# Gated heads: each token's own score from an elementwise product on GpSimd and sums over two columns, in place of whole blocks times the identity

## The chip, the cores and the metric

The kernel runs on one core of a Trainium2 chip. The core has TensorE (matmuls, PE in the profile; its weight loads are PEld), VectorE (DVE), ScalarE (ACT), GpSimd (POOL) and SyncE (SP), which issues DMAs. TensorE writes to PSUM, eight banks of 128 partitions by 2 KB; the other data lie in SBUF. The engines run each their own list of instructions in order and wait for one another through semaphores. The metric is the device time of one execution in microseconds (us), the median of several runs.

## The reference, cut to what matters

The model is a two-layer decoder trunk on 512 tokens and 16 meta tokens (528 rows, width 1024). Each layer has a mixer of four retention heads and four gated heads (GLA, key width 64), then a gated MLP. The change is in the gated heads' scores within a sub-chunk:

```python
ddiff = cs[..., :, None, :] - cs[..., None, :, :]
dec = jnp.exp(jnp.where(causal[:, :, None], ddiff, -jnp.inf))
diag = jnp.einsum('bhnasd,bhnatd,bhnastd->bhnast', qs, ks, dec)
```

A query's score with an earlier key is weighted by the decays that lie between them. For a token with itself the decay is exp(0) = 1, and the score is just the sum over the 64 key elements of q times k, with no gate in it. That score, one number per token and head, is what the change computes in another way.

## The kernel before, in words

Activations are kept transposed: features on the 128 partitions, the 528 tokens along the free dimension. Weights come by DMA into a staging tile (`st`), and each block of 128 columns is split into two fp16 parts, the high one by ScalarE (L122) and the low one by VectorE (L126); both make a `unit`. A projection is 24 matmuls of such units with the fp16 parts of the input (`product_step`, L471 to L473), once for 232 and once for 296 tokens, into a PSUM tile `pj`. ScalarE takes it out (L1018), or for retention's q and k the rotary code on VectorE and ScalarE (L836 to L839).

The gated heads come in two pairs per layer; a pair lies on the 128 partitions as two heads of 64 (k in `kT`, q in `qT`, both in the tile `room`). For each pair `gla` is a generator that `mixer` starts once the last q is there (`done`), and whose pieces are interleaved with the projections: `gla_decay` makes the per-token decay `a` on ScalarE and VectorE (L902 to L909); `gla_scores` makes the scores; `gla_states` and `head_out` make the outputs.

`gla_scores` works in seven levels. The scores of a token with itself come first: for each head, keys against queries of the same 128 tokens as whole 128x128 blocks (`d0`, in PSUM, L955; for the 16 meta tokens `ptl`), of which VectorE keeps the diagonal by a product with the identity (L957 into `dg`, L958 into `dt`). Then q is multiplied by `a` (L960). At every level, token blocks double in length: ScalarE and VectorE write an fp16 split of the tile of keys and queries, `lvx` (L977, L978); GpSimd and VectorE multiply keys and queries by the decay of the neighbouring block (L980, L982); VectorE makes the decay products of the next level in `tots` (L985); TensorE multiplies the level's keys and queries (`lps`, L925), and VectorE copies the results under a mask over their place in `dg` and `dt` (L934, L938).

After the opening of layer 0, Tile's scheduler decides the order of instructions on each engine and inserts the waits. PSUM tiles rotate through the eight banks: `mm` has three buffers, `mx` five, and a matmul into a new tile waits until the last reader of the bank is done. SBUF tiles of 2112 bytes per partition rotate through 41 slots (`g`). `v_natural` transposes the values on TensorE into `ptv` (L746), between the projections.

Of the kernel before, what the change touches and what calls it, by code (L numbers as in the profile page):

```python
# [9 lines left out]
F32 = mybir.dt.float32  # L10
U8 = mybir.dt.uint8
AF = mybir.ActivationFunctionType
ALU = mybir.AluOpType

P = 128
NMETA = 16
SEQ = 512
L = NMETA + SEQ
D = 1024
KD = D // P  # L20
# [34 lines left out]
NROW = 84  # L55
# [20 lines left out]
def cell(pool, shape, dt, tag, name, bufs=None):  # L76

    n = math.prod(shape[1:])
    size = 2 if dt == F16 else 4
    t = pool.tile([shape[0], -(-n * size // CELL) * CELL // size], dt, tag=tag, name=name, **({"bufs": bufs} if bufs else {}))[:, :n]  # L80
    names = "abcdef"[: len(shape) - 1]
    return t if len(names) == 1 else t.rearrange(f"p ({' '.join(names)}) -> p {' '.join(names)}", **dict(zip(names, shape[1:])))
# [136 lines left out]
class Kern:  # L219
# [111 lines left out]

    def constants(self):
        nc, a, c = self.nc, self.a, self.const
        widths = (("h", KD * L), ("xroom", KD * L), ("ident", P), ("ones", P), ("mhalf", 10), ("par", NROW), ("pars", 48), ("cvec", 4 * 88), ("ss", 10), ("first", 10),
                  ("w2", 256), ("rank", KD * 16), ("tri", P), ("mask", len(LEVELS) * 16), ("decay", 2 * NH * 5 + 1), ("sso", 8), ("rooms", sum(n * c for _, n, c in KINDS)))
        every = cell(c, [P, sum(n for _, n in widths)], F32, "every", "every")
        at = 0
        for nm, n in widths:
            setattr(self, nm, every[:, at : at + n])
            at += n  # L340
        self.h = self.h.rearrange("p (k n) -> p k n", k=KD)
        self.mask = self.mask.bitcast(U8).rearrange("p (l c) -> p l c", l=len(LEVELS))
        self.heads = self.decay
        self.decay, self.early = self.heads[:, :-1].rearrange("p (a h c) -> p a h c", a=2, h=NH), self.heads[:, -1:]
        self.ring(self.rooms, KINDS)
        nc.gpsimd.memset(self.ones, 1.0)
        nc.gpsimd.memset(self.mhalf, -0.5)

    def first_gains(self, r0):
        nc = self.nc  # L350
        pt = self.mx([P, 16], "ptc")
        nc.tensor.transpose(pt, r0[:16, :], self.ident[:16, :16])
        nc.vector.tensor_copy(self.par[:, 0:16], pt)
        nc.vector.tensor_scalar(out=self.pars[:, 0:16], in0=pt, scalar1=SX, scalar2=None, op0=ALU.mult)
# [582 lines left out]
                m4 = self.mask[:16, li, :8].rearrange("p (b l) -> p b l", l=lv)  # L937
                nc.vector.copy_predicated(o4, m4, pst.rearrange("p (b l) -> p b l", l=lv))  # L938

    def gla_scores(self, kq, a, res):  # L940

        nc = self.nc
        kT, qT = kq[:, 0, :], kq[:, 1, :]
        dg = [self.g([P, 4, P], F32, "dg") for _ in range(2)]
        dt = self.sm([P, 2, P], "dgt")
        idb = self.ident[:, None, :].to_broadcast([P, 4, P])
        pss, ptl = [self.mx([P, 4, P], "d0") for _ in range(2)], [self.mx([P, 16], "ptl") for _ in range(2)]  # L950
        for c, (c0, w) in enumerate(HEADS):
            for h in range(2):
                hs = slice(64 * h, 64 * h + 64)
                dst = pss[h][:, c - 1, :] if c else ptl[h]
                nc.tensor.matmul(dst, kT[hs, c0 : c0 + P], qT[hs, c0 : c0 + w], start=True, stop=True)  # L955
        for h in range(2):
            nc.vector.tensor_tensor(out=dg[h], in0=pss[h], in1=idb, op=ALU.mult)  # L957
            nc.vector.tensor_tensor(out=dt[:NMETA, h, :NMETA], in0=ptl[h][:NMETA], in1=self.ident[:NMETA, :NMETA], op=ALU.mult)  # L958
        yield
        nc.vector.tensor_tensor(out=qT, in0=qT, in1=a, op=ALU.mult)  # L960
        tots = self.g([P, L], F32, "tots")
        tot, toff = a, 0
        xs = {}
        for step in range(len(LEVELS) + 1):
            if step < len(LEVELS):
                lv = LEVELS[step]
                at = 0 if lv <= 8 else NMETA
                n = L - at
                nb = n // (2 * lv)
                if lv == NMETA:  # L970
                    tot = tot[:, 1:]
                v = lambda t: t.rearrange("p (b two l) -> p b two l", two=2, l=lv)
                x = xs[step] = self.g([P, 2, n], F16, "lvx")
                k0 = v(kT[:, at:])
                p0, b0, t0, l0 = [list(d) for d in k0.ap]
                both = bass.AP(tensor=k0.tensor, offset=k0.offset, ap=[p0, b0, [L + lv, 2], l0])
                nc.scalar.activation(v(x[:, 0]), both, AF.Copy)  # L977
                nc.vector.tensor_tensor(out=v(x[:, 1]), in0=both, in1=v(x[:, 0]), op=ALU.subtract)  # L978
                t2 = tot[:, : n // lv].rearrange("p (b two) -> p b two", two=2)
                nc.gpsimd.tensor_tensor(out=k0[:, :, 0, :], in0=k0[:, :, 0, :], in1=t2[:, :, 1:2].to_broadcast([P, nb, lv]), op=ALU.mult)  # L980
                q1 = v(qT[:, at:])[:, :, 1, :]
                nc.vector.tensor_tensor(out=q1, in0=q1, in1=t2[:, :, 0:1].to_broadcast([P, nb, lv]), op=ALU.mult)  # L982
                tn = tots[:, toff : toff + nb]
                toff += nb
                nc.vector.tensor_tensor(out=tn, in0=t2[:, :, 0], in1=t2[:, :, 1], op=ALU.mult)  # L985
                tot = tn
            if step > 0:
                self.level_scores(step - 1, xs.pop(step - 1), dg, dt)
            yield LEVEL / PACE[0]
        res["kn"], res["tot"] = self.k_natural(kT), tot  # L990
        res["in"] = [lambda i, h=h: dg[h][:, i - 1, :] if i else dt[:, h, :] for h in range(2)]
        yield

    def mixer(self, l):
        nc = self.nc
# [11 lines left out]
        out, vnat, gates = {}, {}, {("gr", h): [None] for h in range(4)} | {("rg", h): [None] for h in range(4)}  # L1007
# [15 lines left out]
        kq = [room[:, 2 * L * pr : 2 * L * (pr + 1)].rearrange("p (i n) -> p i n", i=2) for pr in range(2)]  # L1023
# [4 lines left out]

        def gla(pr):
            res = {}  # L1030
            yield from self.gla_decay(*logits[pr], res)
            if pr:
                yield from self.pause(2)
            yield from self.gla_scores(kq[pr], res["a"], res)
            heads = (2 * pr, 2 * pr + 1)
            yield from self.pause()
            while any(("gv", hd) not in vnat for hd in heads):
                yield "waits"
            yield from self.gla_states(res["kn"], res["tot"], [vnat["gv", hd] for hd in heads], res)
            self.spawn(self.head_out([(res["in"][h], kq[pr][64 * h : 64 * h + 64, 1, :], res["sn"][64 * h : 64 * h + 64], vnat["gv", hd],  # L1040
                                       R_GLA + 4 * l + hd, gates["gr", hd], 4 + hd, None) for h, hd in enumerate(heads)]))
# [16 lines left out]
        def done(nm, h):  # L1058
            if (nm, h) == ("gq", 1):
                logits.extend(self.gate_logits(l, gaT))  # L1060
                self.gated.extend([gla(0), gla(1)])
            elif nm in ("gv", "rv"):
                self.spawn(vtr((nm, h)))
            elif nm == "rq":
                self.spawn(ret(h))
            elif nm in gates_n:
                gates[nm, h][0] = out[nm, h]
# [436 lines left out]
```

## Time and profile before

| | |
|---|---|
| median of 3 runs | 1232.73 us (1232.47 to 1232.76) |
| profiled execution | 1231.38 us |
| its span, first to last instruction | 1229.3 us |
| mean granted TensorE clock | 0.998 |
| busy in the span: TensorE / VectorE / ScalarE / GpSimd | 1209.6 / 869.0 / 676.5 / 161.8 us |

The profile page gives busy times, groups of instructions by line and what they waited for; the timeline gives start and duration of single instructions. A row such as `73.49 0.26 PE L471 MATMUL pj<-every,unit ... x1 [1.18 <-DVE dg L957]` reads: at 73.49 us into the span a matmul of line 471 started, writing the tile pj; the engine had stood idle for 1.18 us, until VectorE's instruction of line 957 was done. Matmuls are pipelined, so what one costs is read from start to start and not from its duration. A matmul in fp32 stands as two records. x16 and the like counts records that follow one another. The four places of the change lie at 67 to 77 us and 83 to 86 us (layer 0) and at 680 to 689 us and 696 to 698 us (layer 1).

### The profile page before, as it was taken

Reading aid. Unit: us, or ns where it says so; the run is one execution under the profiler, and the core shown is the slowest. Engines: PE = TensorE matmul, PEld = TensorE weight load, DVE = VectorE, ACT = ScalarE, POOL = GpSimd, SP = SyncE. Lnnn points to the kernel's source line nnn. Section 1 sums busy time; section 2 is a strip of 40 time slices with the busy share of each in tenths; the row PEclk is TensorE's granted clock in tenths of the full one; section 3 lists DMA queues with packets and bytes.
Section 4 is the critical chain, followed back from the end, with each engine's and each line's share of the span. In section 5 each row is a group of like instructions: output and inputs, shape, how many; then the busy total and the mean of one; then the engine's idle time right before and its main releaser. Section 6 shows DMA issues by size and latency. Waiting matters only on the chain.

```text
span 1229.3 us, 26444 instructions
## 1 busy us (share of the span) xinstructions
PE 1209.6 (98%) x11031; PEld 1012.3 (82%) x11031; DVE 869.0 (71%) x1541; ACT 676.5 (55%) x1337; POOL 161.8 (13%) x211
## 2 busy tenths in 40 slices
PE   8999999999999999999999999999999999999997
PEld 7778889979888888888887788899798888886444
DVE  5677845367998889623465878443779998887686
ACT  6675445454776666523336654453548766664452
POOL 2012311152000000000230123011520000000001
PEclk9999999999999999999999999999999999999999
DMA  8933221131422423424242332212303353305471
GB/s 210 269 103 87 67 73 53 52 103 36 137 70 70 122 86 109 141 80 103 63 113 68 104 87 70 75 48 70 114 8 104 103 172 103 121 1 172 151 251 69
DMA packets 207259, 124.17 MB, mean 101 GB/s; under 512 B 6992, under 2 KB 194692, under 8 KB 207140
## 3 DMA queue, kind: packets, MB, share of 16 engines
q1 hardware_dynamic: 206372, 121.23, 34.0%
q8 instruction: 86, 1.41, 0.5%
q10 hardware_dynamic: 608, 0.73, 0.2%
q0 software_dynamic: 160, 0.52, 0.1%
q14 instruction: 33, 0.27, 0.1%
HBM read 120.37 MB, written 2.10 MB: 100 GB/s over the span
## 4 chain that ended last, share of the span: by engine, by line
PE 82%; DVE 9%; ACT 4%; issue 2%; POOL 1%; DMA 1%; SPq 0%; POOLq 0%; DVEq 0%; ACTq 0%
PE pl L1345 8%; PE pu L472 8%; PE pu L473 8%; PE pu L471 8%; PE pj L471 7%; PE pj L473 7%; PE pj L472 7%; PE pp L1164 5%; PE pd L471 3%; PE pd L473 3%; PE pd L472 3%; PE po L471 2%; PE po L473 2%; PE po L472 2%; DVE unit L126 1%
## 5 line engine op out<-in xcount | busy, mean ns | idle before, releaser
L472 PE MATMUL pu<-every,unit 128*128 128x296 f16 (+2 forms) x1120 | 306.1, 274 | 2.6 <-DVE every L410 2.6
L473 PE MATMUL pu<-every,unit 128*128 128x296 f16 (+2 forms) x1120 | 306.1, 274 | 0.0
L471 PE MATMUL pu<-every,unit 128*128 128x296 f16 (+2 forms) x1120 | 304.5, 274 | 0.7 <-ACT every L409 0.7
L473 PEld LDWEIGHTS <-unit 128*128 128x128 f16 x2572 | 251.7, 98 | 42.0 <-issue 3.4
L471 PEld LDWEIGHTS <-unit 128*128 128x128 f16 x2572 | 252.3, 98 | 41.1 <-issue 3.0
L472 PEld LDWEIGHTS <-unit 128*128 128x128 f16 x2572 | 252.1, 98 | 39.2 <-issue 3.0
L126 DVE SCALAR_TENSOR_TENSOR unit<-st,unit 128x1024 f16<-128x1024 f32 (+1 forms) x165 | 201.6, 1225 | 84.3 <-ACT unit L122 83.7
L471 PE MATMUL pj<-every,unit 128*128 128x296 f16 (+2 forms) x888 | 244.4, 276 | 3.0 <-ACT gv L1018 1.6
L473 PE MATMUL pj<-every,unit 128*128 128x296 f16 (+2 forms) x888 | 244.2, 275 | 0.9 <-DVE unit L126 0.9
L472 PE MATMUL pj<-every,unit 128*128 128x296 f16 (+2 forms) x888 | 244.3, 275 | 0.0
L122 ACT ACTIVATE unit<-st 128x1024 f16<-128x1024 f32 x163 | 169.7, 1042 | 77.5 <-PE pd L473 22.7
L437 DVE TENSOR_TENSOR acc<-acc,sq 128x296 f32<-128x296 f32 (+2 forms) x60 | 32.9, 550 | 75.8 <-ACT sq L435 74.0
L1164 PEld LDWEIGHTS <-unit 128*128 128x128 f16 x756 | 73.9, 98 | 13.3 <-issue 2.3
L473 PE MATMUL pd<-av,unit 128*128 128x232 f16 (+1 forms) x308 | 84.7, 276 | 0.0
L472 PE MATMUL pd<-av,unit 128*128 128x232 f16 (+1 forms) x308 | 84.7, 276 | 0.0
L471 PE MATMUL pd<-av,unit 128*128 128x296 f16 (+1 forms) x308 | 84.5, 276 | 0.0
L1220 ACT ACTIVATE u<-pu 128x296 f32<-128x296 f32 (+2 forms) x140 | 52.5, 378 | 50.2 <-PE pu L473 49.4
L405 POOL TENSOR_TENSOR every<-every 128x5 f32<-128x5 f32 (+6 forms) x31 | 38.1, 1231 | 284.1 <-DVE every L404 244.3
L1345 PE MATMUL pl<-unit,fk 128*128 128x512 f16 x330 | 71.4, 379 | 0.0
L473 PE MATMUL po<-merged,unit 128*128 128x296 f16 (+2 forms) x256 | 69.7, 274 | 0.0
L472 PE MATMUL po<-merged,unit 128*128 128x296 f16 (+2 forms) x256 | 69.7, 274 | 0.0
L1209 DVE SCALAR_TENSOR_TENSOR cg<-u,every,cg 128x527 f32<-128x527 f32 (+1 forms) x88 | 66.2, 752 | 4.7 <-ACT cg L1204 4.3
(272 smaller groups left out, 1899.2 us busy)
## 6 DMA issues: line engine op xcount, KB each, us to landing
st<-in_ffn_up SPq DMA_DIRECT2D x70, 512.0 KB, 3.8
st<-in_w_in SPq DMA_DIRECT2D x56, 512.0 KB, 4.0
st<-in_ffn_down SPq DMA_DIRECT2D x46, 512.0 KB, 4.5
st<-in_ffn_up SPq DMA_DIRECT2D x36, 256.0 KB, 4.0
st<-in_w_out SPq DMA_DIRECT2D x16, 512.0 KB, 4.8
st<-in_ffn_down SPq DMA_DIRECT2D x8, 384.0 KB, 3.6
out<-yo SPq DMA_DIRECT2D x7, 256.0 KB, 2.1
w<-in_ffn_down SPq DMA_DIRECT2D x3, 512.0 KB, 4.6
```

What stands on the lines that cost most here:

```text
L122: self.kern.nc.scalar.activation(self.u[:, 0], self.st, AF.Copy, scale=SW)
L126: self.kern.nc.vector.scalar_tensor_tensor(out=self.u[:, 1, ks], in0=self.st[:, ks], scalar=SW, in1=self.u[:, 0, ks], op0=ALU.mult, op1=AL ...
L405: nc.gpsimd.tensor_tensor(out=r[:w, :n], in0=t[:w, :n], in1=self.mhalf[:w, :n], op=ALU.pow)
L437: eng.tensor_tensor(out=acc[:, :n], in0=acc[:, :n], in1=sq[:, :n], op=ALU.add)
L471: nc.tensor.matmul(ps[:, :n], w[:, 0, kk, :], x[:, 0, n0:n1], start=first, stop=False)
L472: nc.tensor.matmul(ps[:, :n], w[:, 0, kk, :], x[:, 1, n0:n1], start=False, stop=False)
L473: nc.tensor.matmul(ps[:, :n], w[:, 1, kk, :], x[:, 0, n0:n1], start=False, stop=last)
L1164: mm = lambda p, q, **kw: nc.tensor.matmul(ps, u[:, p, k, :], x[k][:, q], skip_group_check=more, **kw)
L1209: nc.vector.scalar_tensor_tensor(out=to, in0=u[:, max(lo, d) - d : L - d], scalar=self.cvec[:, ci(i) : ci(i) + 1], in1=to, op0=ALU.mult, o ...
L1220: nc.scalar.activation(u[:, n0:n1], ps[:, : n1 - n0], AF.Copy, scale=IXW)
L1345: mm = lambda x, w, **kw: nc.tensor.matmul(ps[:, cols], x, w[:, cols], skip_group_check=more, **kw)
```

## The change

The element products of k and q of a pair are made by GpSimd (128x528, fp32, L1032 after the change) as soon as `gla` starts, ahead of the decay, into the tile `tots`, which is therefore taken from its slot earlier. In `gla_scores`, five fp32 matmuls sum them over each head's 64 partitions: the products are the weights (128 columns of tokens; five times), the moving side is `heads2`, two columns of ones and zeros, one for each head. One PSUM tile `own`, 5x2 numbers per partition, holds the result for all blocks and both heads, where two tiles `d0` and two `ptl` stood. VectorE multiplies the identity by these columns, broadcast along the row, into `dg` and `dt`. The product of q and `a` stands ahead of these in the code, and the `yield` behind them. `heads2` is set by three memsets at the start. The scratch for dynamic DMA descriptors is set to 4096 bytes.

```diff
-    def gla_scores(self, kq, a, res):
+    def gla_scores(self, kq, a, tots, res):
...
-        pss, ptl = [self.mx([P, 4, P], "d0") for _ in range(2)], [self.mx([P, 16], "ptl") for _ in range(2)]
+        own = self.mx([P, 5, 2], "own")
         for c, (c0, w) in enumerate(HEADS):
-            for h in range(2):
-                hs = slice(64 * h, 64 * h + 64)
-                dst = pss[h][:, c - 1, :] if c else ptl[h]
-                nc.tensor.matmul(dst, kT[hs, c0 : c0 + P], qT[hs, c0 : c0 + w], start=True, stop=True)
+            nc.tensor.matmul(own[:, c, :], tots[:, c0 : c0 + P], self.heads2, start=True, stop=True)
+        nc.vector.tensor_tensor(out=qT, in0=qT, in1=a, op=ALU.mult)
         for h in range(2):
-            nc.vector.tensor_tensor(out=dg[h], in0=pss[h], in1=idb, op=ALU.mult)
-            nc.vector.tensor_tensor(out=dt[:NMETA, h, :NMETA], in0=ptl[h][:NMETA], in1=self.ident[:NMETA, :NMETA], op=ALU.mult)
-        yield
-        nc.vector.tensor_tensor(out=qT, in0=qT, in1=a, op=ALU.mult)
-        tots = self.g([P, L], F32, "tots")
+            nc.vector.tensor_tensor(out=dg[h], in0=idb, in1=own[:, 1:, h : h + 1].to_broadcast([P, 4, P]), op=ALU.mult)
+        nc.vector.tensor_tensor(out=dt[:NMETA, :, :NMETA], in0=self.ident[:NMETA, None, :NMETA].to_broadcast([NMETA, 2, NMETA]),
+                                in1=own[:NMETA, 0, :, None].to_broadcast([NMETA, 2, NMETA]), op=ALU.mult)
+        yield
         tot, toff = a, 0
...
         def gla(pr):
             res = {}
+            tots = self.g([P, L], F32, "tots")
+            nc.gpsimd.tensor_tensor(out=tots, in0=kq[pr][:, 0, :], in1=kq[pr][:, 1, :], op=ALU.mult)
             yield from self.gla_decay(*logits[pr], res)
...
-    nc = bacc.Bacc("TRN2", target_bir_lowering=False, num_devices=1)
+    nc = bacc.Bacc("TRN2", target_bir_lowering=False, num_devices=1, dynamic_dma_scratch_size=4096)
```

The order of ScalarE's and SyncE's instructions is the same as before. On VectorE, in layer 0 ahead of the first pair's level 0, stood (weight splits into unit, ptl and d0 into room's dt and dg, q times a, decay products in tots, the fp16 split lvx):

```order
L126 SCALAR_TENSOR_TENSOR unit<-st,unit 128x1024 x2
L958 TENSOR_TENSOR room<-ptl,every 16x16 x2
L126 SCALAR_TENSOR_TENSOR unit<-st,unit 128x1024
L957 TENSOR_TENSOR dg<-d_902,every 128x512
L957 TENSOR_TENSOR dg<-d_903,every 128x512
L960 TENSOR_TENSOR room<-room,a 128x528
L985 TENSOR_TENSOR tots<-a 128x264
L985 TENSOR_TENSOR tots<-tots 128x132
L978 TENSOR_TENSOR lvx<-room,lvx 128x528
```

Now there stand, with the line numbers of the changed kernel (L956 is q times a, L958 the product into dg, L959 that into dt):

```order
L126 SCALAR_TENSOR_TENSOR unit<-st,unit 128x1024 x2
L956 TENSOR_TENSOR room<-room,a 128x528 x2
L985 TENSOR_TENSOR tots<-a 128x264
L958 TENSOR_TENSOR dg<-every,own 128x512 x2
L959 TENSOR_TENSOR room<-every,own 16x2x16
L126 SCALAR_TENSOR_TENSOR unit<-st,unit 128x1024
L985 TENSOR_TENSOR tots<-tots 128x132
L978 TENSOR_TENSOR lvx<-room,lvx 128x528
```

The product of q and a of the second pair has moved up beside the first pair's, and the third weight split has moved behind the products into dg and dt. In layer 1 the rows are the same, except that one more L126 stands between L956 and L985.

On TensorE, in layer 0 at the second pair (ptl and d are the old scores, ptv a transpose of values, pj a projection), stood:

```order
L473 MATMUL pj<-every,unit 128x232
L955 MATMUL ptl<-room 128x16 x2
L955 MATMUL d_1138<-room 128x128
L955 MATMUL d_1139<-room 128x128
L955 MATMUL d_1138<-room 128x128
L955 MATMUL d_1139<-room 128x128
L955 MATMUL d_1138<-room 128x128
L955 MATMUL d_1139<-room 128x128
L955 MATMUL d_1138<-room 128x128
L955 MATMUL d_1139<-room 128x128
L746 MATMUL ptv_1158<-every,gv 128x128
```

Now there stand:

```order
L476 MATMUL pj<-every,unit 128x232
L955 MATMUL own<-every,tots 128x2 x5
L749 MATMUL ptv_1147<-every,gv 128x128
L749 MATMUL ptv<-every,gv 128x128 x4
L474 LDWEIGHTS unit
L474 MATMUL pj<-every,unit 128x296
```

Ten matmuls have become five, and the four other transposes have moved up to the first one. At the three other places the ten become five in the same way and nothing else moves on TensorE.

More of the change, by code (lines that the diff above doesn't have):

```diff
@@ L333, in constants @@
         nc, a, c = self.nc, self.a, self.const
-        widths = (("h", KD * L), ("xroom", KD * L), ("ident", P), ("ones", P), ("mhalf", 10), ("par", NROW), ("pars", 48), ("cvec", 4 * 88), ("ss", 10), ("first", 10),
+        widths = (("h", KD * L), ("xroom", KD * L), ("ident", P), ("ones", P), ("mhalf", 10), ("heads2", 2), ("par", NROW), ("pars", 48), ("cvec", 4 * 88), ("ss", 10), ("first", 10),
                   ("w2", 256), ("rank", KD * 16), ("tri", P), ("mask", len(LEVELS) * 16), ("decay", 2 * NH * 5 + 1), ("sso", 8), ("rooms", sum(n * c for _, n, c in KINDS)))
@@ L347, in constants @@
         nc.gpsimd.memset(self.mhalf, -0.5)
+        nc.gpsimd.memset(self.heads2, 0.0)
+        for h in range(2):
+            nc.gpsimd.memset(self.heads2[64 * h : 64 * h + 64, h : h + 1], 1.0)
     def first_gains(self, r0):
@@ L1033, in gla @@
                 yield from self.pause(2)
-            yield from self.gla_scores(kq[pr], res["a"], res)
+            yield from self.gla_scores(kq[pr], res["a"], tots, res)
             heads = (2 * pr, 2 * pr + 1)
```

## The prediction, on record before the changed kernel ran

> **What bounds the kernel now.** I read the page's busy times first, then TensorE's list of waits, then the timelines of the four places where the gated heads make their own scores.
>
> ```profile
> PE 1209.6 (98%) x11031; PEld 1012.3 (82%) x11031; DVE 869.0 (71%) x1541; ACT 676.5 (55%) x1337; POOL 161.8 (13%) x211
> ```
>
> TensorE is busy for all but 20 us of a span of 1229.3, so only what leaves its stream, or what it stands waiting for, is worth time. Its waits inside layer 0's mixer (60 to 200 us), its weight loads' wait there, and then the same two of layer 1's mixer (680 to 840 us):
>
> ```profile
> PE pj L471 <- DVE dg L957: 1.2, 1, 1.2
> PE lps L925 <- DVE lvx L978: 0.3, 1, 0.3
> PEld L471 <- DVE room L938: 0.4, 1, 0.4
> PE pj L471 <- ACT gv L1018: 1.6, 1, 1.6
> PEld L471 <- DVE room L938: 0.3, 1, 0.3
> ```
>
> Three of these stand behind the matmuls that the change removes. In the timeline of TensorE, layer 0 first and then layer 1 (start, duration, instruction; in brackets the idle time before it):
>
> ```profile
> 68.57 0.30 PE L471 MATMUL pj<-every,unit 128*128 128x296 f16 x1
> 71.60 0.71 PE L746 MATMUL ptv<-every,gv 128*128 128x128 f32 x5
> 73.49 0.26 PE L471 MATMUL pj<-every,unit 128*128 128x232 f16 x1 [1.18 <-DVE dg L957]
> 76.47 0.58 PE L925 MATMUL lps<-lvx 64*128 64x8 f16 x28 [0.34 <-DVE lvx L978]
> ```
>
> ```profile
> 682.63 0.29 PE L471 MATMUL pj<-every,unit 128*128 128x296 f16 x1 [1.63 <-ACT gv L1018]
> 685.65 0.71 PE L746 MATMUL ptv<-every,gv 128*128 128x128 f32 x5
> 686.19 0.26 PE L471 MATMUL pj<-every,unit 128*128 128x232 f16 x1
> 688.67 0.52 PE L925 MATMUL lps<-lvx 64*128 64x8 f16 x24
> ```
>
> A projection has no use for dg: it waits 1.18 us because its PSUM bank was that of the block scores d0, which VectorE had not yet multiplied. The 1.63 us of layer 1 come at the same step, for a bank that ScalarE still held. So the four PSUM tiles of the old scores cost waits beside their matmuls. What comes next is lvx of level 0, the first tile that the level matmuls need.
>
> **What the matmuls cost, and what replaces them.** Layer 0's second pair, where TensorE waits for nothing around them:
>
> ```profile
> 83.75 0.26 PE L473 MATMUL pj<-every,unit 128*128 128x232 f16 x1
> 83.95 0.40 PE L955 MATMUL ptl<-room 64*128 64x16 f32 x4
> 84.19 1.14 PE L955 MATMUL d<-room 64*128 64x128 f32 x16
> 85.26 0.33 PE L746 MATMUL ptv<-every,gv 128*128 128x128 f32 x1
> ```
>
> From 83.75 to 85.26 is 1.51; less the slot of the projection's last matmul, 0.10 (24 of them take 686.19 to 688.67), a pair costs 1.41. Five fp32 matmuls of 128 rows, 128 columns of weights and two moving columns come instead. No row shows that form. Its neighbours are the sums of squares (99 columns of weights, one moving column) and the retention scores (128 columns, 128 moving):
>
> ```profile
> 296.32 0.60 PE L421 MATMUL nst<-every,acc 128*99 128x1 f32 x6
> 296.79 0.26 PE L472 MATMUL pu<-every,unit 128*128 128x232 f16 x1
> ```
>
> ```profile
> 101.11 1.14 PE L849 MATMUL rs<-rq,rk 128*128 128x128 f32 x8
> 102.09 0.60 PE L764 MATMUL ptk<-every,rk 128*128 128x128 f32 x4
> ```
>
> Three of the first take 0.47, so five take 0.78: the floor, as 128 columns load no faster than 99. Four of the second take 0.98, so five take 1.23: the ceiling. I take 1.0, in the middle: the moving side is like the first row, the loaded side like the second. A pair saves 0.41 (0.18 to 0.63).
>
> The Trainium skill (TensorE: Matmul & The Clock Gate, section LDWEIGHTS) says that a load costs its columns divided by 1.2 ns whatever the moving side, which speaks against narrow products; ten loads of 128 would be an estimated 1.07, a pair would save 0.34, and the sum below would be 3.0 in place of 3.1. The 99-column row, 0.078 per record where the rule gives 0.083, agrees.
>
> **The first pairs: VectorE's order decides.** There the saving on TensorE is worth nothing by itself, since lvx ends the wait. VectorE's rows, layer 0 and then layer 1:
>
> ```profile
> 69.29 1.23 DVE L126 SCALAR_TENSOR_TENSOR unit<-st,unit 128x1024 f16<-128x1024 f32 x1 [3.58 <-ACT unit L122]
> 71.61 1.23 DVE L126 SCALAR_TENSOR_TENSOR unit<-st,unit 128x1024 f16<-128x1024 f32 x1 [0.94 <-ACT unit L122]
> 72.75 1.28 DVE L957 TENSOR_TENSOR dg<-d,every 128x512 f32<-128x512 f32 x2
> 73.95 0.69 DVE L960 TENSOR_TENSOR room<-room,a 128x528 f32<-128x528 f32 x1
> 74.57 0.42 DVE L985 TENSOR_TENSOR tots<-a 128x264 f32<-128x264 f32 x1
> 75.02 0.29 DVE L985 TENSOR_TENSOR tots<-tots 128x132 f32<-128x132 f32 x1
> 75.59 0.83 DVE L978 TENSOR_TENSOR lvx<-room,lvx 128x528 f16<-128x528 f32 x1 [0.28 <-ACT lvx L977]
> ```
>
> ```profile
> 680.00 1.23 DVE L126 SCALAR_TENSOR_TENSOR unit<-st,unit 128x1024 f16<-128x1024 f32 x1 [3.58 <-ACT unit L122]
> 682.31 1.23 DVE L126 SCALAR_TENSOR_TENSOR unit<-st,unit 128x1024 f16<-128x1024 f32 x1 [1.09 <-ACT unit L122]
> 687.59 0.84 DVE L978 TENSOR_TENSOR lvx<-room,lvx 128x528 f16<-128x528 f32 x1 [0.27 <-ACT lvx L977]
> ```
>
> Before the second weight split VectorE sits idle for about a microsecond, waiting for ScalarE. By the new order both pairs' products of q and a stand in that gap, and behind them L985, the two dg products and the split. ScalarE's decays a of both pairs are there by then (the last pieces, layer 0 and layer 1):
>
> ```profile
> 69.16 1.16 ACT L909 ACTIVATE a<-a 128x528 f32<-128x528 f32 x2
> ```
>
> ```profile
> 680.17 1.17 ACT L909 ACTIVATE a<-a 128x528 f32<-128x528 f32 x2
> ```
>
> Steps from start to start: split 1.14 (71.61 to 72.75), dg 0.60 (half of 72.75 to 73.95), q times a 0.62, L985 0.45, the small dt product 0.12 (an assumption: no row has 16x32), L985 of 132 columns 0.29, lvx 0.83. Layer 0: 69.29 + 1.14 = 70.43 (a ends at 70.32, so no wait), + 2 x 0.62 + 0.45 + 2 x 0.60 + 0.12 + 1.14 + 0.29 + 0.83 = 75.70. It ended at 76.42, and TensorE went on 0.05 later. TensorE would be there at 68.57 - 0.41 + 3.03 + 0.54 + 2.48 = 74.2 (24 matmuls from 68.57 to 71.60, transposes from 685.65 to 686.19, 24 narrower matmuls from 686.19 to 688.67), so it waits 1.5 for lvx in place of 1.18 and 0.34, and goes on 0.72 earlier. Layer 1 has one more split in the row: 680.00 + 1.14 + 2 x 0.62 + 1.14 + 0.45 + 1.20 + 0.12 + 1.14 + 0.29 + 0.84 = 687.56. TensorE came at 688.67, having waited 1.63; now it would come at about 686.6 and go on at 687.61: 1.06 earlier.
>
> **The rest.** After this the weight loads' wait for the copies of L938 (0.4 and 0.3, of which some 0.1 is the usual load) goes too: one small PSUM tile stands where four stood, so the projection behind the second transposes no longer takes a bank that those copies read. 0.25 per layer; what comes next, the rotary products of VectorE, moves forward with lvx. If they are late instead, this term is nothing.
>
> The GpSimd products: 128x528 in fp32, two per layer. Its nearest row has 296 columns:
>
> ```profile
> L452 POOL TENSOR_TENSOR every<-every,tmp 128x296 f32<-128x296 f32 x24 | 21.8, 947 | 10.3 <-DVE tmp L450 10.3
> ```
>
> Layer 0's last q on ScalarE, and a GpSimd product beside which VectorE runs:
>
> ```profile
> 57.50 0.42 ACT L1018 ACTIVATE room<-pj 128x296 f32<-128x296 f32 x1 [1.66 <-PE pj L473]
> 76.57 1.08 POOL L980 TENSOR_TENSOR room<-room,a 128x264 f32<-128x264 f32 x1 [25.13 <-DVE tots L985]
> 76.82 0.87 DVE L985 TENSOR_TENSOR tots<-tots 128x33 f32<-128x33 f32 x1
> ```
>
> 528 / 296 x 0.947 = 1.7; by L980's 1.08 for 264 columns, 2.2. The last q is there at 57.92, so both are done by 62 at the latest, and GpSimd is idle until 76.57. The scores are wanted at 67.2 (68.57 - 1.41), so the products cost nothing, with five microseconds of cover; were that gone, all of TensorE's stream would wait behind own, microsecond for microsecond. The dt products, the three memsets at the start and the two longer-lived slots are taken at nothing. The smaller DMA scratch touches the two GpSimd DMAs alone, 74 us ahead of their first use (the second row has the first and the last start):
>
> ```profile
> 1119.05 1.30 POOL L1333 DMA_DIRECT2D every<-in_post_ffn_norm  x2 [213.27 <-DVE ca L1209]
> ```
>
> ```profile
> L1366 DVE SCALAR_TENSOR_TENSOR yo<-yo,every x6: 678/682/686, 1193.0 to 1211.1; 128x512 f32<-128x512 f32 x6
> ```
>
> **The sum.** Layer 0: 0.72 + 0.25 + 0.41 = 1.38. Layer 1: 1.06 + 0.25 + 0.41 = 1.72. Together 3.1 us, with nothing else in TensorE's stream changed. The profiled execution took 1231.38; it would take 1228.3. The median of the three runs is 1.35 higher, 1232.73, so I forecast 1229.6 for the median. What a measurement can tell from no change is 0.2%, or 2.5 us: below 1230.3 is faster.
>
> Bounds: the matmuls 0.78 to 1.23 each shift the second pairs by 0.22 each. The dg products read one PSUM column over and over, which no row shows; as short as L985's 0.42 they would give 0.36 more per layer, and at twice 0.60 they take 1.2 per layer. Ends: 3.1 + 0.45 + 0.7 + some 0.2 = 4.5, or 1228.2; 3.1 - 0.45 - 2.1 = 0.6, or 1232.1.
>
> **Rivals.**
> - The waits only change their names: lvx comes no earlier, since the products of both pairs, the dt product and the split run into one another, and the first pairs gain nothing. For: VectorE's order puts five steps ahead of the split that used to be one. Against: it was idle for 0.94 there. Left are 2 x 0.41 + 2 x 0.25 = 1.3: 1231.4, no change that can be told.
> - The GpSimd products hold up VectorE. For: L985 took 0.87 beside L980, where its wider neighbour took 0.29 alone. If a layer's two products hold the gate's chain for half of their 1.7 each, 1.7 per layer is lost, 3.4 against 3.1: 1233.0, no change that can be told. Against: the chain then waits for ScalarE, and a ends ten microseconds later. The Trainium skill (GPSIMD Engine Reference, Specifications) says that the two share their SBUF interfaces when VectorE has two SBUF inputs; L985's row agrees.
> - Slower: a dg product with a broadcast PSUM column takes 2.5 us, four times 0.60. Then lvx comes 3.8 later in each layer, and TensorE's wait with it: 7.6 - 3.1 = 4.5 more, 1237.2. It turns at 1.4 us per product. Against: the level products broadcast a column from SBUF and show no such price.
> That the change fails to do what it says is no case: in the order the old matmuls are gone.
>
> **Chances.** Forecast 0.60, of which 0.07 falls short of 0.2%; the first rival 0.26; the second 0.08; the slower one 0.06. So faster 0.53, within 0.2% 0.41, slower 0.06. The range 1228.2 to 1232.1 holds the forecast and the first rival.
>
> **What would show it.** L955 as five matmuls of about 1.0 us per pair; no wait at the two pj; a wait of 1 to 1.5 us at the first lps of each layer, ended by lvx at 75.7 and 687.6 less the shift of layer 0 (1.4); dg at 0.60 each; GpSimd's products done by 62. Wrong would be: lvx at its old place, a wait at own for GpSimd, or the gain lost again between 110 and 640 us, where nothing is changed.

## The result, and the profile after

| | before | after |
|---|---|---|
| median | 1232.47 us (7 runs, 1231.12 to 1232.76) | 1227.53 us (7 runs, 1227.10 to 1229.67) |
| ratio, 95% interval | | 0.9968 (0.9958 to 0.9978) |
| profiled execution, span | 1231.38, 1229.3 us | 1227.53, 1225.6 us |
| mean granted TensorE clock | 0.998 | 0.999 |

The ratio is 3.9 us of 1232 (2.7 to 5.2), where 3.1 was forecast. The median itself, 1227.53, lies 0.7 below the lower end of the range (1228.2); the ratio, taken from the 1232.73 that the forecast started from, gives 1228.8, which lies in it. A second timing of the same kernel gave 0.9970 (0.9958 to 0.9982). The first row of the page, and then the one wait of TensorE that is left in the gated heads' scores:

```profile
PE 1207.8 (99%) x10991; PEld 1012.6 (83%) x10991; DVE 869.2 (71%) x1537; ACT 675.9 (55%) x1337; POOL 171.0 (14%) x218
```

```profile
PE lps L928 <- DVE lvx L978: 1.4, 2, 1.1
```

TensorE's busy time fell by 1.8 us and the span by 3.7: about half was matmuls, and half was standing still. The waits at the two pj (1.2 and 1.6 us) are gone, and so are the weight loads' waits for the copies into dt. What came in their place is a wait for lvx, 1.10 us in layer 0 and 0.34 in layer 1. TensorE's timeline (start, duration, instruction, idle time before it), layer 0 and then layer 1:

```profile
57.14 0.77 PE L893 MATMUL z<-gaT,every 32*128 32x296 f32 x4
...
66.91 1.17 PE L955 MATMUL own<-every,tots 128*128 128x2 f32 x10
67.95 0.29 PE L474 MATMUL pj<-every,unit 128*128 128x296 f16 x1
75.26 0.58 PE L928 MATMUL lps<-lvx 64*128 64x8 f16 x28 [1.10 <-DVE lvx L978]
75.77 0.77 PE L749 MATMUL ptv<-every,gv 128*128 128x128 f32 x5
82.32 1.19 PE L955 MATMUL own<-every,tots 128*128 128x2 f32 x10
83.36 0.74 PE L749 MATMUL ptv<-every,gv 128*128 128x128 f32 x5
87.06 0.61 PE L928 MATMUL lps<-lvx 64*128 64x8 f16 x30
...
677.63 1.17 PE L955 MATMUL own<-every,tots 128*128 128x2 f32 x10
685.23 0.58 PE L928 MATMUL lps<-lvx 64*128 64x8 f16 x28 [0.34 <-DVE lvx L978]
```

TensorE's wait for lvx was forecast at 1 to 1.5 us in each layer; it is that in layer 0 and shorter in layer 1. own takes 1.04 us from its start to the next instruction's (66.91 to 67.95, 82.32 to 83.36). VectorE on its way to the first lvx of layer 0, and the last step of that way in layer 1:

```profile
69.04 1.22 DVE L126 SCALAR_TENSOR_TENSOR unit<-st,unit 128x1024 f16<-128x1024 f32 x1 [3.58 <-ACT unit L122]
70.18 1.32 DVE L956 TENSOR_TENSOR room<-room,a 128x528 f32<-128x528 f32 x2
71.42 0.42 DVE L985 TENSOR_TENSOR tots<-a 128x264 f32<-128x264 f32 x1
71.76 1.28 DVE L958 TENSOR_TENSOR dg<-every,own 128x512 f32<-128x512 f32 x2
72.96 0.17 DVE L959 TENSOR_TENSOR room<-every,own 16x32 f32<-16x32 f32 x1
73.06 1.21 DVE L126 SCALAR_TENSOR_TENSOR unit<-st,unit 128x1024 f16<-128x1024 f32 x1
74.19 0.28 DVE L985 TENSOR_TENSOR tots<-tots 128x132 f32<-128x132 f32 x1
74.40 0.81 DVE L978 TENSOR_TENSOR lvx<-room,lvx 128x528 f16<-128x528 f32 x1
...
684.36 0.81 DVE L978 TENSOR_TENSOR lvx<-room,lvx 128x528 f16<-128x528 f32 x1
```

From 69.04 to 75.21 VectorE runs without a gap: the microsecond in which it used to wait for ScalarE is filled. lvx ends at 75.21, and 0.05 us later TensorE goes on.

**How the runs below are compared.** In some profiled executions the granted clock dips just ahead of layer 1, where no kernel was changed. The same stretch of the changed kernel and of the kernel q_copy below, and then three single microseconds of q_copy (stretch, its length, busy time and count of each engine, PE clock, DMA):

```profile
640.00:676.00 36.00, 34.47 (x297) 28.43 (x294) 21.45 (x40) 22.99 (x43) 9.66 (x8) 1.00 0.28 74
```

```profile
640.00:676.00 36.00, 34.47 (x289) 28.23 (x287) 21.77 (x42) 21.04 (x41) 8.70 (x9) 0.95 0.29 79
654.00:655.00 1.00, 0.43 (x3) 0.29 (x3) 1.00 (x4) 1.00 (x4) 0.00 (x0) 1.00 0.00 0
657.00:658.00 1.00, 1.00 (x6) 0.60 (x5) 1.00 (x4) 0.33 (x1) 0.00 (x0) 0.50 0.00 0
659.00:660.00 1.00, 1.00 (x10) 0.78 (x9) 1.00 (x4) 0.43 (x1) 0.00 (x0) 1.00 0.00 0
```

The 0.95 is a mean over 36 us: for some 3.4 us, from about 655.5 to 659, the clock is at half, and at 1.00 on both sides. That makes 1.7 us. TensorE stands still twice there, for 0.87 us up to 654.57 and for 0.66 up to 655.76; in the changed kernel's profile it stands as long, and the clock stays at 1.00, so what decides is not shown. From the second pair's first lps in layer 0 to the own or ptl of layer 1 takes 590.6 us in the changed kernel and 592.3 to 592.5 in the profiled executions of q_copy, first_pairs, second_pairs and product_on_vectore, so their spans say little. I therefore read each effect from a starting point near by. A0 and B0 are counted from the start of z (57.14 above) to the start of the transposes behind the first pair's first lps (75.77), and to the second pair's first lps (87.06). A1 and B1 are the same two in layer 1, from the start of the first pair's own or ptl. With the same code these four agree within 0.02 us from kernel to kernel; the one exception is A1, and with it B1, of the kernel before, where the wait for gv was 1.63 us in one execution and 1.39 in another (A1 9.59 and 9.35). The second timings of the changed kernel and of dg_behind repeat the four within 0.01.

| kernel | median, us | ratio to before (95%) | A0 | B0 | A1 | B1 |
|---|---|---|---|---|---|---|
| before | 1232.47 | | 19.60 | 31.59 | 9.59 | 21.52 |
| changed | 1227.53 | 0.9968 (0.9958 to 0.9978) | 18.63 | 29.92 | 8.11 | 19.40 |
| first_pairs | 1228.41 | 0.9976 (0.9967 to 0.9985) | 18.01 | 29.69 | 8.04 | 20.18 |
| second_pairs | 1230.11 | 0.9988 (0.9979 to 0.9997) | 19.65 | 30.94 | 9.34 | 20.63 |
| q_copy | 1231.66 | 0.9995 (0.9986 to 1.0003) | 18.69 | 31.17 | 9.34 | 21.02 |
| dg_gpsimd | 1228.80 | 0.9978 (0.9969 to 0.9987) | 19.10 | 30.39 | 8.83 | 20.12 |
| own_twice_first | 1227.54 | 0.9969 (0.9958 to 0.9981) | 18.65 | 29.94 | 8.11 | 19.39 |
| own_twice_second | 1228.64 | 0.9974 (0.9963 to 0.9985) | 18.63 | 31.04 | 8.10 | 19.39 |
| lvx_twice | 1228.46 | 0.9972 (0.9960 to 0.9983) | 18.64 | 29.93 | 8.97 | 20.26 |
| product_on_vectore | 1228.71 | 0.9974 (0.9964 to 0.9984) | 18.64 | 29.93 | 8.11 | 19.39 |
| scratch_alone | 1231.67 | 1.0001 (0.9992 to 1.0009) | 19.61 | 31.59 | 9.35 | 21.27 |
| dg_behind | 1227.64 | 0.9959 (0.9946 to 0.9973) | 17.38 | 29.00 | 7.61 | 19.16 |

Each ratio is taken against runs of the kernel before from the same set. Their medians differ from set to set (1232.47 for the changed kernel, 1231.61 from first_pairs to dg_gpsimd, 1231.45 for own_twice, lvx_twice and dg_behind, 1231.25 for product_on_vectore and scratch_alone), so the medians of two rows can be compared only within a set. The 3.7 us by which the changed kernel's span is shorter can be placed with them: 1.67 up to B0, 2.12 up to B1, 0.25 ahead of z and 0.07 between the two layers, less 0.4 that are lost again behind B1.

The theory to be tested: in the first pairs the gain is VectorE's earlier lvx together with the banks that are no longer held, and matmul time is worth nothing there; in the second pairs it is matmul time and the copies' wait. The rival: the gain is matmul time alone, the same in each of the four pairs.

### The profile page after: what moved, and what is told of

Read it like the earlier page. It is cut to its first block, busy times and chain, and to the rows that moved or that the text cites. A ratio compares the mean times of both kernels' runs of the same rounds, so it can differ in the third digit from the quotient of the medians.

```text
span 1225.6 us, 26383 instructions
## 1 busy us (share of the span) xinstructions
PE 1207.8 (99%) x10991; PEld 1012.6 (83%) x10991; DVE 869.2 (71%) x1537; ACT 675.9 (55%) x1337; POOL 171.0 (14%) x218
## 3 DMA queue, kind: packets, MB, share of 16 engines
q8 instruction: 86, 1.41, 0.5%
## 4 chain that ended last, share of the span: by engine, by line
PE 77%; DVE 12%; ACT 5%; issue 3%; DMA 1%; POOL 1%; SPq 0%; DVEq 0%; POOLq 0%; ACTq 0%
PE pu L475 8%; PE pu L476 8%; PE pu L474 8%; PE pj L474 7%; PE pj L476 7%; PE pj L475 7%; PE pp L1166 5%; PE pd L475 3%; PE pd L474 3%; PE pd L476 3%; PE pl L1347 2%; PE po L475 2%; PE po L474 2%; PE po L476 2%; DVE unit L126 2%
## 5 line engine op out<-in xcount | busy, mean ns | idle before, releaser
L126 DVE SCALAR_TENSOR_TENSOR unit<-st,unit 128x1024 f16<-128x1024 f32 (+1 forms) x165 | 202.3, 1229 | 81.8 <-ACT unit L122 81.1
```

Source lines behind the costliest of these rows:

```text
L126: self.kern.nc.vector.scalar_tensor_tensor(out=self.u[:, 1, ks], in0=self.st[:, ks], scalar=SW, in1=self.u[:, 0, ks], op0=ALU.mult, op1=AL ...
```

## The experiments

**One half of the change at a time: first_pairs and second_pairs.** A flag for the pair chooses between the new scores and the old blocks.

```diff
-            tots = self.g([P, L], F32, "tots")
-            nc.gpsimd.tensor_tensor(out=tots, in0=kq[pr][:, 0, :], in1=kq[pr][:, 1, :], op=ALU.mult)
+            tots = self.g([P, L], F32, "tots") if pr == 0 else None      # second_pairs: pr == 1
+            if pr == 0:
+                nc.gpsimd.tensor_tensor(out=tots, in0=kq[pr][:, 0, :], in1=kq[pr][:, 1, :], op=ALU.mult)
```

> The new scores for the first pair of each layer, the old blocks for the second. Theory (the first pairs gain by VectorE's earlier lvx and by the PSUM banks that are free, the second pairs by TensorE's shorter matmuls and the wait of the copies): the larger part of the changed kernel's 3.9 us stays. Layer 0: TensorE goes on about 1.0 to 1.5 us earlier at the first lps, layer 1 about 1.3 to 1.6 us earlier; time 2.3 to 3.1 us below before, that is 0.8 to 1.6 above the changed kernel. Rival (the gain is matmul time alone, the same for each of four pairs): 2.0 below before, and the waits at pj and lps together as long as before.

> The new scores for the second pair of each layer, the old blocks for the first. Theory: 0.37 per pair of matmul time (1.41 less 1.04) and 0.25 to 0.3 per pair for the wait of the copies of the 16-token part: 1.2 to 1.4 us below before; the waits at the first pairs' pj (1.2 and 1.6 us) stay. Rival (an equal share of the gain in each pair): 2.0 below before.

TensorE in first_pairs:

```profile
75.20 0.58 PE L928 MATMUL lps<-lvx 64*128 64x8 f16 x28 [0.47 <-DVE lvx L992]
...
692.48 0.27 PE L474 MATMUL pj<-every,unit 128*128 128x232 f16 x1 [0.28 <-DVE room L941]
```

VectorE there, q times a with the step behind it in layer 0, and the split behind it in layer 1:

```profile
70.74 0.70 DVE L957 TENSOR_TENSOR room<-room,a 128x528 f32<-128x528 f32 x1
71.36 0.43 DVE L999 TENSOR_TENSOR tots<-a 128x264 f32<-128x264 f32 x1
...
682.36 1.22 DVE L126 SCALAR_TENSOR_TENSOR unit<-st,unit 128x1024 f16<-128x1024 f32 x1 [0.47 <-ACT unit L122]
```

And in second_pairs:

```profile
73.48 0.26 PE L474 MATMUL pj<-every,unit 128*128 128x232 f16 x1 [1.17 <-DVE dg L971]
683.45 0.29 PE L474 MATMUL pj<-every,unit 128*128 128x296 f16 x1 [1.39 <-ACT gv L1032]
```

The shares are not equal. first_pairs is 3.0 us under before (0.0024 of 1232; 1.8 to 4.1), second_pairs 1.5 (0.4 to 2.6); the rival's 2.0 lies in both intervals, so the times alone don't settle it, and the distances do. With the new scores in the first pairs alone, A0 falls by 1.59 and A1 by 1.31 to 1.55; with them in the second pairs alone both pj waits stand where they were, A0 and A1 hardly move (19.65 beside 19.60, 9.34 beside 9.35), and the way from A to B falls from 11.99 to 11.29 in layer 0 and from 11.93 to 11.29 in layer 1, exactly as in the changed kernel. The theory's numbers hold, but for A0, which it put at 1.0 to 1.5. The surprise is in layer 0: first_pairs brings A0 0.62 lower than the whole change does, because the second pair's q times a (0.62 us on VectorE) no longer runs ahead of the first pair's lvx. In the changed kernel that step is in the way. At B0 first_pairs is still 0.23 lower: with the first pair's new scores in place, the second pair's cost layer 0 time on balance, at least up to there. In layer 1 the step costs next to nothing (A1 8.04 beside 8.11), since VectorE would wait there for ScalarE. Nor do the halves simply add up in the copies' wait: from A to B first_pairs takes 11.68 in layer 0, so that wait goes with the first pairs alone too, and 12.14 in layer 1, where TensorE itself now waits for a copy into dt (the last row of its timeline).

**The freed order alone: q_copy.** The old blocks, but from a copy of q (and the scratch of the changed kernel):

```diff
+            tots = self.g([P, L], F32, "tots")
+            nc.gpsimd.tensor_copy(tots, kq[pr][:, 1, :])
...
-                nc.tensor.matmul(dst, kT[hs, c0 : c0 + P], qT[hs, c0 : c0 + w], start=True, stop=True)
+                nc.tensor.matmul(dst, kT[hs, c0 : c0 + P], tots[hs, c0 : c0 + w], start=True, stop=True)
+        nc.vector.tensor_tensor(out=qT, in0=qT, in1=a, op=ALU.mult)
```

> The kernel before, but its old blocks read a copy of q that GpSimd makes, so that q times a doesn't wait for TensorE's matmuls and can stand ahead of the second weight split, as in the changed kernel; matmuls and PSUM tiles as before. Theory (the freed order on VectorE is worth nothing by itself, since the projection behind the first pair still waits for the bank that the first dg product reads, and that product now comes later, behind both products of q and a): layer 0 waits at pj 1.2 to 1.8 us, and TensorE reaches the first lps no earlier than before; time from 0.5 us below to 1.0 us above before. Rival (the freed order alone makes the first pairs' gain): lvx about 1.1 us earlier and the time 1.8 to 2.2 us below before.

TensorE:

```profile
75.55 0.58 PE L925 MATMUL lps<-lvx 64*128 64x8 f16 x28 [0.76 <-DVE lvx L977]
80.54 0.66 PE L746 MATMUL ptv<-every,gv 128*128 128x128 f32 x4 [0.58 <-ACT vn L748]
...
683.75 0.29 PE L471 MATMUL pj<-every,unit 128*128 128x296 f16 x1 [1.38 <-ACT gv L1017]
```

The time came out about as the theory said (0.6 us under before, 1.7 under to 0.4 above), but in layer 0 not by the way that it gave. The wait at pj did not stay: the projection started at 72.13, ahead of VectorE's dg products (73.49 to 74.69), so its bank was no longer theirs, and A0 fell by 0.91. Half of it was given back at once, at a transpose that now had to wait 0.58 us for ScalarE's vn, so that B0 is 0.42 lower only. In layer 1 the projection still waits for gv's bank, and A1 is that of scratch_alone; B1 is 0.25 lower, as the weight loads' wait for the copies (0.3) is gone. So the early q times a by itself is worth 0.7 us of the 3.5 that the distances show for the whole change beside scratch_alone; with the old blocks and their four PSUM tiles other waits take its place. That the change needs the early q times a is argued from VectorE's rows; no run here leaves it out.

**Is matmul time worth anything? own_twice_first and own_twice_second.** The same extra work at two places:

```diff
         for c, (c0, w) in enumerate(HEADS):
-            nc.tensor.matmul(own[:, c, :], tots[:, c0 : c0 + P], self.heads2, start=True, stop=True)
+            for _ in range(2 if flag else 1):      # flag: layer 0, first pair; or layer 0, second pair
+                nc.tensor.matmul(own[:, c, :], tots[:, c0 : c0 + P], self.heads2, start=True, stop=True)
```

> The changed kernel with the five matmuls of own issued twice in the first pair of layer 0 alone (1.04 us more for TensorE). Theory (there TensorE waits 1.10 us for lvx, so matmul time is worth nothing in a first pair): the first lps starts within 0.1 us of its place in the changed kernel, the wait ahead of it falls from 1.10 to 0.1, and the time is the same within 0.2 us. Rival (matmul time counts in every pair): 1.04 us more, at the lps and at the end.

> The changed kernel with the five matmuls of own issued twice in the second pair of layer 0 alone. Theory (in a second pair TensorE waits for nothing): everything behind it comes 1.04 us later, the second pair's first lps and the end alike. Rival (the extra 1.04 us is hidden by a wait that would stand behind it anyway): under 0.3 us.

The first:

```profile
66.91 2.29 PE L956 MATMUL own<-every,tots 128*128 128x2 f32 x20
75.09 0.75 PE L928 MATMUL lps<-lvx 64*128 64x8 f16 x30
```

The second:

```profile
82.32 2.30 PE L956 MATMUL own<-every,tots 128*128 128x2 f32 x20
84.48 0.74 PE L749 MATMUL ptv<-every,gv 128*128 128x128 f32 x5
88.18 0.61 PE L928 MATMUL lps<-lvx 64*128 64x8 f16 x30
```

Doubling adds 1.12 us to own (84.48 less 83.36). In the first pair nothing of it arrives: the wait for lvx is eaten up, A0 and B0 are those of the changed kernel within 0.02. In the second pair all of it arrives, B0 is 1.12 higher; in the medians, taken in one set, it is 1.1 (1227.54 and 1228.64). Both halves of the theory hold, and the rival falls.

**Is lvx what TensorE waits for? lvx_twice.**

```diff
-                nc.vector.tensor_tensor(out=v(x[:, 1]), in0=both, in1=v(x[:, 0]), op=ALU.subtract)
+                for _ in range(2 if flag and step == 0 else 1):      # flag: layer 1, first pair
+                    nc.vector.tensor_tensor(out=v(x[:, 1]), in0=both, in1=v(x[:, 0]), op=ALU.subtract)
```

> The changed kernel with VectorE's fp16 split of the first level (L978, 128x528) made twice in the first pair of layer 1 alone. The second one stands behind the decay product of 66 columns, so lvx ends 0.73 + 0.14 = 0.9 us later. Theory (lvx is what TensorE waits for): the wait at the first lps of layer 1 grows from 0.34 to about 1.2 us, and the time by 0.9 us. Rival (the wait there is a name only, and another release comes as late): the wait grows by less than 0.4 us, and the time is the same.

TensorE:

```profile
686.03 0.58 PE L928 MATMUL lps<-lvx 64*128 64x8 f16 x28 [1.20 <-DVE lvx L979]
```

The wait went from 0.34 to 1.20, and A1 and B1 are 0.86 higher. In layer 1 too, every tenth that VectorE is late is a tenth of TensorE's.

**What GpSimd's part costs: product_on_vectore and scratch_alone.** The first makes the products of k and q with `nc.vector` in place of `nc.gpsimd`; the second adds the scratch size to the kernel before.

> The changed kernel with the products of k and q (L1032, 128x528) on VectorE instead of GpSimd; VectorE takes them between weight splits, about 0.6 us each. Theory (GpSimd's products cost nothing in the changed kernel, and VectorE's would lie in stretches where it is ahead of TensorE): the time is within 0.5 us of the changed kernel, and VectorE's instructions beside the products are no shorter than before. Rival (GpSimd's products, like its dg products in the kernel with those moved there, make VectorE's work beside them longer by up to a microsecond each and this reaches TensorE): the time is 0.5 to 2 us below the changed kernel.

> The kernel before with the scratch for dynamic DMA descriptors at 4096 bytes and nothing else changed; the instructions stand in the same order. Theory (it touches two GpSimd DMAs alone, far ahead of their use): within 0.5 us of before. Rival (some of the changed kernel's gain that is not found in the four pairs comes from it): 0.5 to 1 us below before.

GpSimd's products in the changed kernel, and VectorE's splits beside them:

```profile
54.73 1.30 POOL L1032 TENSOR_TENSOR tots<-room 128x528 f32<-128x528 f32 x1 [2.34 <-ACT room L1018]
57.74 1.33 POOL L1032 TENSOR_TENSOR tots<-room 128x528 f32<-128x528 f32 x1 [1.71 <-ACT room L1018]
```

```profile
55.62 1.49 DVE L126 SCALAR_TENSOR_TENSOR unit<-st,unit 128x1024 f16<-128x1024 f32 x1 [1.79 <-ACT unit L122]
58.64 1.51 DVE L126 SCALAR_TENSOR_TENSOR unit<-st,unit 128x1024 f16<-128x1024 f32 x1 [1.53 <-ACT unit L122]
```

Two splits take 1.49 and 1.51 us where they take 1.23 before and with the products on VectorE; but VectorE waits for ScalarE later anyway, 3.58 us ahead of its split at 69.04. With the products on VectorE the four distances are the changed kernel's within 0.01, and the two ratios overlap: the choice of engine is worth nothing here. scratch_alone stands at before's B0, and its ratio is 1.0001 (0.9992 to 1.0009): the scratch costs and brings nothing that these runs can tell.

**Can the wait that is left be taken away? dg_gpsimd and dg_behind.** Both move the first pair's dg and dt products out of VectorE's way to lvx: the one to GpSimd, from sums that VectorE copies out of PSUM; the other to behind lvx, from sums that ScalarE copies.

```diff
+            sums = self.sm([P, 5, 2], "owns")
+            nc.vector.tensor_copy(sums, own)                  # dg_gpsimd: then dg, dt by nc.gpsimd
...
+                    nc.scalar.activation(sums, own, AF.Copy)  # dg_behind: then dg, dt by nc.vector, behind step 0
```

> The changed kernel, with the first pairs' products into dg and dt on GpSimd, from sums that VectorE copies out of PSUM (128x10). Theory (VectorE's chain to the first lvx sets when TensorE goes on; 1.3 us of products leave it): lvx ends at 74.0 in layer 0 in place of 75.2, the waits of 1.1 and 0.3 us at the first lps go, and the time is 1.0 to 1.4 us below the changed kernel. Rival (GpSimd's products, 1.3 to 2.0 us each, run beside VectorE's split and lvx and make them longer, or hold up GpSimd's products of the next level): a wait of the same length stands at the first or the second lps, and the time is within 0.5 us of the changed kernel or above it.

VectorE in dg_gpsimd, and GpSimd beside it:

```profile
73.30 1.14 DVE L989 TENSOR_TENSOR tots<-tots 128x132 f32<-128x132 f32 x1
74.36 1.63 DVE L982 TENSOR_TENSOR lvx<-room,lvx 128x528 f16<-128x528 f32 x1
...
682.85 2.09 DVE L126 SCALAR_TENSOR_TENSOR unit<-st,unit 128x1024 f16<-128x1024 f32 x1
```

```profile
72.33 3.01 POOL L962 TENSOR_TENSOR dg<-every,owns 128x512 f32<-128x512 f32 x2 [12.94 <-DVE owns L958]
```

The theory fell and the rival stood: 1.3 us of work left VectorE, and two other instructions in each layer became 0.82 to 0.87 us longer: those of 0.28, 0.81 and 1.22 us in the rows, and in layer 1 one of 0.21, which took 1.07. lvx ends at 75.99, A0 is 0.47 and A1 0.72 higher than in the changed kernel. The Trainium skill (SBUF — State Buffer, section "SBUF: two separate sides") says that GpSimd and a VectorE instruction with two SBUF inputs hold one port pair in turn, each for its whole instruction; the rows agree, since all of them read two SBUF tiles; and the GpSimd product that comes behind the start of a weight split takes 1.96 us in layer 0 and 2.03 in layer 1, the other one 1.09 and 1.05.

> The changed kernel, but in the first pairs ScalarE copies the sums out of PSUM (128x10, behind its L977), and VectorE makes dg and dt from that copy behind lvx instead of ahead of it. GpSimd is not used for it, so there is no contention. Theory (what VectorE has ahead of the first lvx sets when TensorE goes on): lvx ends 1.2 us earlier, at 74.0 in layer 0, the waits of 1.10 and 0.34 us at the first lps go to nothing or to under 0.2, and the time is 1.0 to 1.4 us below the changed kernel. Rival (VectorE's work behind lvx, now 1.3 us later, is what TensorE needs next: the weight split, or the copies that free the banks): a wait of 0.5 to 1.2 us appears at a pj or ptv between 76 and 84 us, and the time is within 0.5 us of the changed kernel.

> The changed kernel itself, timed once more beside the next kernel on the same chip. Theory and rival alike: 3.5 to 4.5 us below before; it is here as the base for the next one.

> The kernel with the first pairs' dg and dt products behind lvx, timed once more. Theory (of the 1.25 and 0.5 us by which the first run's trace showed TensorE earlier in the first pairs, 0.33 and 0.26 are given back in the second pairs): 0.5 to 1.2 us below the changed kernel timed beside it. Rival (the two are the same): within 0.3 us.

TensorE and then VectorE in dg_behind:

```profile
74.22 0.60 PE L928 MATMUL lps<-lvx 64*128 64x8 f16 x30
79.26 0.26 PE L474 MATMUL pj<-every,unit 128*128 128x232 f16 x1 [0.17 <-ACT tmp L841]
```

```profile
73.35 0.82 DVE L982 TENSOR_TENSOR lvx<-room,lvx 128x528 f16<-128x528 f32 x1
74.08 1.28 DVE L993 TENSOR_TENSOR dg<-every,owns 128x512 f32<-128x512 f32 x2
```

Here the wait for lvx is gone in both layers: lvx ends at 74.17, and TensorE goes on without a stop. A0 is 1.25 and A1 0.50 lower than in the changed kernel; 0.33 and 0.26 are given back before the second pair, where a projection waits 0.17 us for ScalarE's tmp, and 0.92 and 0.24 are left. In the times this is hard to see. The second timing of both gave medians of 1227.98 (5 runs) and 1228.04 (6 runs of the changed kernel), fastest runs of 1226.78 and 1227.39, and ratios of 0.9964 (0.9952 to 0.9977) and 0.9970 (0.9958 to 0.9982). dg_behind may be half a microsecond better; these runs cannot tell it from the changed kernel.

The spans of these two differ by 0.5 us where the four distances promise 1.16. Behind B1 the rest takes 528.2 us in changed_again and 528.9 in dg_behind_again. TensorE keeps its lead nearly to its end (its last row of matmuls starts at 1216.63 and 1215.58), but the chain that ended last does not run over TensorE there. In both it runs from 1150 us on over ScalarE's and VectorE's splits of the last weights, and through one DMA of these weights, first in changed_again and then in dg_behind_again (start, duration):

```profile
1180.54 7.02 DMA st<-in_ffn_down
```

```profile
1179.36 7.69 DMA st<-in_ffn_down
```

The DMA starts 1.18 us earlier and takes 0.67 longer, and 0.5 is left. In the profile of before this chain runs over TensorE's matmuls; in that of the changed kernel it runs over such a DMA too, of 7.44 us. So at the end of this kernel a microsecond of TensorE's is no longer a microsecond of the time.

## Why the prediction was right

The forecast of 1229.6 lies 2.1 us above the median of 1227.53. Of that, 0.8 is the sum (3.9 by the ratio, 3.1 forecast; in the distances, 1.67 for layer 0 where 1.38 was forecast, and 1.87 to 2.12 for layer 1 where it was 1.72); the rest is in the medians, which move from one set of runs to the next (before: 1232.73, 1232.47, 1231.61, 1231.45, 1231.25, 1231.72). By its steps:

- **The old scores at 1.41 us and own at 1.0.** own was 1.04, so a pair saves 0.37 and not 0.41. own_twice_second shows that it counts in the second pairs, own_twice_first that it doesn't in the first pair of layer 0, where TensorE has 1.10 us to spare (layer 1, with 0.34 to spare, was not tried). By the Trainium skill (TensorE: Matmul & The Clock Gate, section LDWEIGHTS) ten loads were an estimated 1.07; the rows agree.
- **First pairs: lvx decides.** Right in mechanism, by lvx_twice and own_twice_first. TensorE was to go on 0.72 and 1.06 earlier; it was 0.97, and 1.24 to 1.48 by which of the two executions of before one takes. The term was too small because two steps were set too long: L985 of 264 columns took 0.34 and not 0.45, that of 132 columns 0.21 and not 0.29; with the dt product (0.10 for 0.12), the split and lvx this makes 0.24 of the difference in layer 0, all of it, and 0.26 in layer 1. There TensorE's wait for lvx was to be 1.0 us and was 0.34: lvx ended 7.54 us behind the start of the scores where the working puts it 7.94 behind, and TensorE had two matmuls of lps to do ahead of the wait. A step length taken from a row behind which the engine waits, or from a duration, is longer than the distance to the next start in a full queue.
- **The copies' wait, 0.25 per layer.** B less A fell by 0.70 and 0.64; without 0.37 for the matmuls that leaves 0.33 and 0.27. first_pairs and q_copy show that it doesn't hang on the second pair's tiles alone: it went in layer 0 of the one and in both layers of the other, whose tiles are the old ones.
- **GpSimd's products cost nothing.** Right, by product_on_vectore. They took 1.3 to 2.0 us and were done by 59.1 us.
- **Rivals.** That the waits only change their names was wrong: 3.1 us of TensorE's waits, and 0.7 of its weight loads', became 1.4. That GpSimd holds up VectorE is real as a mechanism (0.27 us on two splits), and in dg_gpsimd it decides; in the change it fell where VectorE was ahead. A dg product with a broadcast PSUM column took 0.60 per step and not 2.5.
- **The upper end of the range.** The working takes off 2.1 for dg products of twice the length, where its own 1.2 per layer makes 2.4; the end would be 1232.5 and not 1232.1. With 0.60 measured it bears on nothing.

Where the reasoning was incomplete: it called q times a of both pairs a filling for VectorE's gap. In layer 0 the second pair's is on the path, and costs 0.62 us there (first_pairs). And it took TensorE for the limit of the whole kernel: behind 1150 us the splits of the last weights and a DMA end the changed kernel.

## What to carry to other kernels

Ask of each matmul that is saved whether the engine would have waited behind it anyway: here the same 1.1 us was worth nothing in one pair and its full price in the next. When TensorE waits for a tile, write down what the engine that makes it does before, in order, and move what is not needed yet to behind it; an idle neighbour is a good place only if it doesn't stretch the instructions that stay. When an engine has become faster, look again at what ends the kernel: here it is a DMA and the splits of the last weights. Where the clock can dip by itself, compare two kernels by distances from a near starting point, and let the medians confirm it.

## What the runs showed of the hardware

- GpSimd's fp32 products (128x512, 1.0 to 2.0 us each) stretch VectorE instructions with two SBUF inputs beside them by 0.82 to 0.87 us, whatever their own length: 0.21 became 1.07, 0.28 became 1.14, 0.81 became 1.63, 1.22 became 2.09.
- Five fp32 matmuls with two moving columns take 1.04 us; five more right behind them add 1.12.
- The granted clock of one core alone fell to half for some 3.4 us ahead of layer 1 in some executions and not in others of like kernels, which makes 1.7 us, nearly half of what this change brings.
